# Seven products for three pairs in the second feed-forward's first group, with a new head, tail and addresses

## The chip, the core and the metric

The kernel runs on one core of a Trainium2 chip. A core has five engines that run side by side, each through its own list of instructions in order: PE (TensorE, matrix products), DVE (VectorE), ACT (ScalarE), POOL (GpSimd) and SP (SyncE, which here only issues DMAs). They meet by semaphores: an instruction waits until others have counted far enough, and everything behind it in its engine's list waits too. The metric is the device time of one execution in microseconds (us). Lines are written L288 for line 288 of the kernel before.

## The reference

One encoder layer on x of 256 tokens by 2048 features, all in float32:

```python
x = x + 0.5 * swiglu_ffn(rms_norm(x, ffn1_norm), ffn1_w_in, ffn1_w_out)
h = rms_norm(x, mix_norm); p = h @ w_mix_in          # convolution group | gated group
x = x + concat(rms(conv_group(p)), rms(gated_group(p))) @ w_mix_out
x = x + memory_cross_attention(rms_norm(x, xattn_norm), rms_norm(mem, mem_norm), w_q, w_kv, w_o)
x = x + 0.5 * swiglu_ffn(rms_norm(x, ffn2_norm), ffn2_w_in, ffn2_w_out)
return rms_norm(x, final_norm)

def swiglu_ffn(h, w_in, w_out):                      # w_in 2048 x 11264, w_out 5632 x 2048
    gate, up = split(h @ w_in, 2)
    return (silu(gate) * up) @ w_out
```

What is to be known of it here: the last product of the attention is o @ w_o; its result is added to x, and then the second feed-forward begins, whose first product needs the normalised x. The normalisation divides each token by the root of its mean square, so the division can be done after the product, on the result.

## The kernel before

*Products.* A float32 product is made of three fast ones. Each weight tile of 128 x 1024 comes by DMA into `raw` (512 KB), ACT rounds it into the high half of `hl` (the cast, L339 in the feed-forwards, L112 elsewhere), DVE subtracts that from the tile into the low half (L340, L113), and x is split in the same way into `x_hl`. The product is high by high, low by high and high by low, added up in PSUM. `raw` has four buffers and `hl` three; the feed-forwards add two more `hl` in a tile `ring`, and five more raws in a tile `spare`.

*A feed-forward* (class `FeedForward`) makes h in 11 groups of 512 gate and 512 up columns. A group goes over 16 steps of k, 128 features each, two to a pair p. In a pair marked C, `eight` makes 24 matmuls of 128 x 512 (`by_two`: two token halves, two column halves, three parts, two steps). In a pair marked S, `seven` makes a product of two by two blocks with seven block products in place of eight: 21 matmuls. It needs sums of weight blocks, which DVE makes (L388, L389, L394, L401) and which are then cast like a weight, and sums of x blocks, the forms, which `sides` makes once (two scalings L368 on ACT, four small operations L370 to L375 on DVE, a cast and a subtraction, L120 and L121). A group's pattern is SCSCSCCC. The seven block products are combined at the end of the third S pair (a copy of block product 1 on ACT, L439, and four additions on DVE, L440 to L443) and of the group. Three steps of k in each group take a weight tile `hl_s` whose low half a DMA on POOL's queue adds up (`summed`, L358 and L359).

*The first group* of each feed-forward does not follow the pattern: it goes through all 16 steps as `by_two` does, 192 matmuls, and beside it `sides` makes the forms at k = 6, 9 and 12. At k = 13 the root of the mean square is made (`rms_cols` and `inverse_root`, with a load of another function table on ACT, L204), and then the table for Silu is loaded again.

*The head.* In the first feed-forward, x comes in transposed pieces (L532), weights in raws, the constants `pv` in two pieces, and x once more in four chunks of 512 KB, which ACT squares in place (L525) in raw buffers at k = 5, 7, 9 and 11.

*Attention's last product.* For f = 0 to 15 (128 features each) `gemm_t` makes o @ w_o, of which parts for f = 0 to 3 were begun before, and `residual` adds it to x on DVE (L251, twice), scales the result by the norm's gain into `x_hl` (L239 on ACT, L240 on DVE) and adds up its squares (L212 or L215, L216). o lies in a tile `o_hl` with the tag S2; `spare` of the second feed-forward has the same tag, so the same room.

*The end.* The last product of the second feed-forward is made token half by token half; `add_up` adds and squares, and `give` makes the root from the four sums of squares and scales and stores the half.

*Order.* The order on each engine is set when the kernel is built, by a scheduler with its own estimates of time, from the dependences between tiles and the order in which the program is written. `issue_after` in the program holds an instruction back in it.

## Time and profile before

| what | value |
| --- | --- |
| runs | 2108.7, 2107.7 and 2108.14 us; median 2108.14 |
| profiled execution | 2108.84 us, of which the span of the profile is 2107.04 |
| mean granted clock of PE | 0.998 |
| busy | PE 2084.5 us (99%), DVE 1576.8 (75%), ACT 1161.6 (55%), POOL 67.7 (3%) |
| matmuls recorded | 9764 |
| bytes moved by DMA | 442.34 MB, 210 GB/s over the span |
| stages | first feed-forward's first group from 7.1 to about 57 us, attention's last product until 1386.3, second feed-forward's first group until about 1430, last matmul at 2096.6 |

In the rows that follow, a time at a row's start is in us from the beginning of the span. A row of a timeline gives start, busy time, engine, line, operation, output and inputs, shape, count, and in brackets how long the engine was idle before it and what released it. A row of a window table gives for each engine busy time and count, then the granted clock, the share of the DMA engines' time and GB/s. A row of groups gives count, busy us and mean ns of one.

### The profile page before, as it was taken

What the parts mean: (1) busy time and instruction counts of PE and PEld (TensorE: products, weight loads), DVE (VectorE), ACT (ScalarE), POOL (GpSimd) and SP (SyncE); (2) the same over time, 40 slices, a digit from 0 to 9 for tenths busy, and PEclk for the clock granted to TensorE, in tenths of its full rate; (3) what the DMA queues carried; (4) which work ended last, traced back from release to release, by engine and by line L of the source; (5) the groups of instructions that cost most, each with busy time, mean ns of one, the idle gap of its engine ahead of it and who ended that gap; (6) DMA issues with size and microseconds to landing.
All of it is one profiled execution on the core that took longest, in us unless ns stands there. A gap on an engine that the chain in (4) does not pass through costs nothing.

```text
span 2107.0 us, 26590 instructions
## 1 busy us (share of the span) xinstructions
PE 2084.5 (99%) x9764; PEld 1738.5 (83%) x9764; DVE 1576.8 (75%) x2215; ACT 1161.6 (55%) x1450; POOL 67.7 (3%) x83
## 2 busy tenths in 40 slices
PE   8999999999999999999999999999999999999998
PEld 6888888888888888888888888888888888888886
DVE  6888888876655589889877665777888887787754
ACT  7666566645544454445665454556665666554443
POOL 0000000000000000000000000000000000000000
PEclk9999999999999999999999999999999999999999
DMA  9778777855666676666565543686787778556664
GB/s 360 230 227 257 229 238 245 263 167 169 216 198 188 206 236 200 190 176 185 176 201 185 186 154 111 206 281 191 231 259 247 232 229 250 178 160 202 197 192 149
DMA packets 122244, 442.34 MB, mean 210 GB/s; under 512 B 13697, under 2 KB 13825, under 8 KB 121729
## 3 DMA queue, kind: packets, MB, share of 16 engines
q1 hardware_dynamic: 113184, 407.35, 58.8%
q0 software_dynamic: 8640, 32.51, 8.5%
q8 instruction: 76, 1.25, 0.2%
q10 hardware_dynamic: 288, 0.79, 0.1%
q14 instruction: 56, 0.45, 0.1%
HBM read 438.49 MB, written 2.10 MB: 209 GB/s over the span
## 4 chain that ended last, share of the span: by engine, by line
PE 84%; issue 11%; DMA 2%; ACT 1%; POOL 1%; DVE 1%; SPq 0%; POOLq 0%; ACTq 0%
PE acc L172 12%; PE acc L173 12%; PE acc L171 12%; PE acc L125 9%; PE acc L289 7%; PE acc L288 7%; PE acc L291 7%; PE acc L126 4%; PE acc L277 2%; PE acc L276 2%; PE acc L275 2%; PE aux L263 1%; PE acc L1066 1%; PE acc L1065 1%; PE acc L1067 1%
## 5 line engine op out<-in xcount | busy, mean ns | idle before, releaser
L113 DVE TENSOR_TENSOR hl<-raw,hl 128x1024 fp32r<-128x1024 f32 (+1 forms) x402 | 488.6, 1216 | 282.5 <-ACT hl L112 281.1
L112 ACT CAST hl<-raw 128x1024 fp32r<-128x1024 f32 (+1 forms) x402 | 419.7, 1045 | 481.6 <-PE acc L173 289.3
L339 ACT CAST hl<-spare 128x1024 fp32r<-128x1024 f32 (+1 forms) x135 | 131.8, 993 | 95.5 <-DVE spare L389 38.5
L340 DVE TENSOR_TENSOR hl<-spare,hl 128x1024 fp32r<-128x1024 f32 (+1 forms) x135 | 154.4, 1150 | 35.8 <-ACT hl L339 34.2
L288 PE MATMUL acc<-hl,x_hl 128*128 128x512 f32 x408 | 144.2, 394 | 9.7 <-ACT hl L339 9.7
L289 PE MATMUL acc<-hl,x_hl 128*128 128x512 f32 x408 | 149.9, 395 | 0.0
L340 DVE TENSOR_TENSOR hl<-raw,hl 128x1024 fp32r<-128x1024 f32 (+1 forms) x101 | 113.9, 1131 | 45.9 <-ACT hl L339 44.3
L339 ACT CAST ring<-spare 128x1024 fp32r<-128x1024 f32 (+1 forms) x99 | 97.2, 988 | 68.9 <-DVE spare L389 26.9
L340 DVE TENSOR_TENSOR ring<-spare,ring 128x1024 fp32r<-128x1024 f32 (+1 forms) x99 | 112.9, 1145 | 19.9 <-ACT ring L339 18.8
L291 PE MATMUL acc<-hl,x_hl 128*128 128x512 f32 x408 | 127.5, 392 | 0.0
L339 ACT CAST hl<-raw 128x1024 fp32r<-128x1024 f32 (+1 forms) x101 | 97.7, 977 | 51.8 <-PE acc L291 16.1
L172 PE MATMUL acc<-hl,x_hl 128*128 128x512 f32 x256 | 100.5, 392 | 0.2 <-DVE hl L113 0.2
L172 PE MATMUL acc<-hl,m_hl 128*128 128x512 f32 x256 | 100.4, 392 | 0.0
L173 PE MATMUL acc<-hl,m_hl 128*128 128x512 f32 x256 | 100.2, 391 | 0.0
L173 PE MATMUL acc<-hl,x_hl 128*128 128x512 f32 x256 | 99.8, 390 | 0.0
L288 PEld LDWEIGHTS acc<-hl,x_hl 128*128 128x128 f32 x408 | 76.8, 189 | 25.9 <-ACT hl L339 10.1
L289 PE MATMUL acc<-ring,x_hl 128*128 128x512 f32 x248 | 93.1, 389 | 0.0
L288 PE MATMUL acc<-ring,x_hl 128*128 128x512 f32 x248 | 91.2, 390 | 0.0
L171 PE MATMUL acc<-hl,m_hl 128*128 128x512 f32 x256 | 91.2, 393 | 0.0
L289 PEld LDWEIGHTS acc<-hl,x_hl 128*128 128x128 f32 x408 | 77.2, 190 | 16.9 <-DVE hl L340 1.1
L291 PEld LDWEIGHTS acc<-hl,x_hl 128*128 128x128 f32 x408 | 77.5, 190 | 16.4
L125 PE MATMUL acc<-x_hl,hl 128*128 128x512 f32 x256 | 91.0, 398 | 0.0
(359 smaller groups left out, 5173.9 us busy)
## 6 DMA issues: line engine op xcount, KB each, us to landing
spare<-in_ffn_w_in SPq DMA_DIRECT2D x192, 512.0 KB, 6.4
raw<-in_ffn_w_out SPq DMA_DIRECT2D x176, 512.0 KB, 3.8
raw<-in_ffn_w_in SPq DMA_DIRECT2D x160, 512.0 KB, 6.3
hl_s<-in_ffn_w_in POOLq DMA_DIRECT2D x44, 512.0 KB, 7.3
raw<-in_w_mix_vg SPq DMA_DIRECT2D x32, 512.0 KB, 4.6
raw<-in_w_k SPq DMA_DIRECT2D x32, 512.0 KB, 4.0
raw<-in_w_v SPq DMA_DIRECT2D x32, 512.0 KB, 4.4
raw<-in_w_mix_out SPq DMA_DIRECT2D x32, 512.0 KB, 4.6
```

The source lines that it names most:

```text
L112: nc.scalar.copy(out=hl[:, 0, :size], in_=raw[:, :size])
L113: newest[0] = nc.vector.tensor_tensor(out=hl[:, 1, :size], in0=raw[:, :size], in1=hl[:, 0, :size].bitcast(F32), op=ALU.subtract)
L125: nc.tensor.matmul(acc, lhsT=w_hi, rhs=x_hl, start=first, stop=False, skip_group_check=True)
L126: nc.tensor.matmul(acc[:, 0], lhsT=w_lo, rhs=x_hl[:, 0], start=False, stop=last, skip_group_check=True)
L171: nc.tensor.matmul(acc[t], lhsT=x[:, 0, s], rhs=hi[:, k], start=k0 + k == 0, stop=False)
L172: nc.tensor.matmul(acc[t], lhsT=x[:, 0, s], rhs=lo[:, k], start=False, stop=False)
L173: nc.tensor.matmul(acc[t], lhsT=x[:, 1, s], rhs=hi[:, k], start=False, stop=k0 + k == nk - 1)
L288: nc.tensor.matmul(acc[t][g], lhsT=x[:, 0, s], rhs=hi[:, cols[g]], start=(t, g) in first, stop=False)
L289: nc.tensor.matmul(acc[t][g], lhsT=x[:, 0, s], rhs=lo[:, cols[g]], start=False, stop=False)
L291: nc.tensor.matmul(acc[t][g], lhsT=x[:, 1, s], rhs=hi[:, cols[g]], start=False, stop=last)
L339: nc.scalar.copy(out=hl[:, 0, :n], in_=raw[:, :n])
L340: newest[0] = nc.vector.tensor_tensor(out=hl[:, 1, :n], in0=raw[:, :n], in1=hl[:, 0, :n].bitcast(F32), op=ALU.subtract)
```

## The change

The changed kernel differs in four things.

1. *First group of the second feed-forward.* It is made by `group(0, ...)`, as the others are: three S pairs of 21 matmuls in place of 24. The root comes inside it, before the last pair. The forms are now made beside attention's last product, at f = 1, 5 and 9, in a `wraw` buffer; the tile `ring` is allocated there.
2. *Head.* The first feed-forward's gains and the first 128 features of x come in one DMA on ACT's queue, the first weight tile in two halves; eleven matmuls of ones run on PE before the first real one. The chunks of x to be squared go into tiles h7 to h4 at k = 2, 4, 6 and 8.
3. *Tail.* Three of the four sums of squares are added up ahead of the last product; in `give` the sum of four and one tensor operation with a small operand are replaced.
4. *Addresses and buffers.* `pv` is 64 bytes shorter, and with small fillers all large tiles (x_hl, ring, spare, raw, hl, h0 to h7) begin at 0 mod 128 where they began at 64. The sums of weight tiles have raw buffers of their own, taken out of the ring of raws (9 become 8, later 7), and are issued after the next step's cast.

Line numbers in the rows of the changed kernel are its own: L372 and L373 are cast and subtraction in the feed-forwards, L115 and L116 elsewhere, L252 and L253 the gain, L225 and L228 the squares, L265 the residual, L323 to L328 the forms, L409, L410, L415 and L422 the sums of weight blocks, L468 to L472 the combination, L392 and L393 the passes for `hl_s`, L217 the root.

ACT's list where attention's last product begins its f loop, in the kernel before (the L112 of 512 is for f = 2, the two of 1024 behind it for f = 3 and 4):

```order
L120 CAST o_hl<-acc 128x256 x4
L112 CAST hl<-raw 128x512
L112 CAST hl<-raw 128x1024 x2
L239 ACTIVATE x_hl<-xT,pv 128x256
L212 ACTIVATE ss<-xT 128x256
L112 CAST hl<-raw 128x1024
L239 ACTIVATE x_hl<-xT,pv 128x256
L215 ACTIVATE sq<-xT 128x256
```

The same place in the changed kernel, ACT:

```order
L123 CAST o_hl<-acc 128x256 x4
L252 ACTIVATE x_hl<-xT,pv 128x256
L225 ACTIVATE ss<-xT 128x256
L323 ACTIVATE raw<-xT,pv 128x256
L252 ACTIVATE x_hl<-xT,pv 128x256
L228 ACTIVATE sq<-xT 128x256
L323 ACTIVATE raw<-xT,pv 128x256
L115 CAST hl<-raw 128x512
L115 CAST hl<-raw 128x1024
L123 CAST ring<-raw 128x4x128
```

Gain, squares and form of f = 0 and of f = 1 now stand ahead of the cast for f = 2.

DVE's list at the end of the last product and the beginning of the second feed-forward, in the kernel before:

```order
L240 SCALAR_TENSOR_TENSOR x_hl<-xT,pv,x_hl 128x256
L216 TENSOR_TENSOR ss<-ss,sq 128x256
L340 TENSOR_TENSOR ring<-raw,ring 128x1024
L340 TENSOR_TENSOR hl<-raw,hl 128x1024
L251 SCALAR_TENSOR_TENSOR xT<-acc,xT 128x256 x2
L340 TENSOR_TENSOR hl<-raw,hl 128x1024
```

And in the changed kernel, DVE (the two L265 are the residual of f = 15, `spare` is the tile in o_hl's room):

```order
L373 TENSOR_TENSOR ring<-raw,ring 128x1024
L253 SCALAR_TENSOR_TENSOR x_hl<-xT,pv,x_hl 128x256
L229 TENSOR_TENSOR ss<-ss,sq 128x256
L265 SCALAR_TENSOR_TENSOR xT<-acc,xT 128x256
L409 TENSOR_TENSOR spare<-raw 128x512
L410 TENSOR_TENSOR spare<-raw 128x512
L265 SCALAR_TENSOR_TENSOR xT<-acc,xT 128x256
L415 TENSOR_TENSOR raw<-spare,raw 128x512
L373 TENSOR_TENSOR hl<-spare,hl 128x1024
```

Where plain low halves stood ready, the first weight sums now stand behind the residual of f = 15, and the cast of these sums is what PE's first products of the group wait for.

ACT's list around the root in the second feed-forward's first group, in the kernel before:

```order
L339 CAST ring<-spare 128x1024 x2
L339 CAST hl<-spare 128x1024 x3
L339 CAST ring<-raw 128x1024
L204 ACT_TABLE_LOAD
L204 ACTIVATE rt_11374<-rv_11373 128x2
L339 CAST ring<-raw 128x512
L418 ACT_TABLE_LOAD
```

And in the changed kernel, ACT (L468 is the copy of block product 1 of the third S pair; the first `ring<-raw` behind it is the cast of that pair's second weight tile):

```order
L372 CAST ring<-raw 128x1024
L372 CAST ring<-spare 128x512
L468 COPY spare<-acc 128x512
L372 CAST ring<-spare 128x1024
L372 CAST ring<-raw 128x1024
L217 ACT_TABLE_LOAD
L217 ACTIVATE rt_11417<-rv_11416 128x2
L372 CAST ring<-spare 128x1024
L372 CAST hl<-raw 128x512
L372 CAST hl<-raw 128x1024 x2
```

The copy and the table load now stand among the casts of the third S pair.

The core of the diff:

```diff
+    gx = xt.tile([P, 2 * KD + KD * T], F32, name="gx", tag="x")
+    gains, xT = gx[:, KD:2 * KD], gx[:, 2 * KD:].rearrange("p (k t) -> p k t", t=T)
+    nc.scalar.dma_start(out=gx[:, KD:2 * KD + T], in_=a["gains_x0"])
+    nc.scalar.dma_start(out=xT[:, 1], in_=a["xT"][:, 1])
+    nc.vector.memset(ones, 1.0)
+    idle = pa.tile([P, 2, T], F32, name="aux")
+    for _ in range(WARM):
+        nc.tensor.matmul(idle[:, 0, :P], lhsT=ones, rhs=ones, start=True, stop=True)
...
             self.raws = [spare[:, i * 1024:(i + 1) * 1024] for i in (5, 0, 1, 2, 3)]
+            self.raws_summed = [self.raws.pop()]
...
         def summed(self, at):
-            raw, hl = self.raw(j, k), self.hls[at % len(self.hls)]
+            raw, hl = self.raws_summed[at % len(self.hls)], self.hls[at % len(self.hls)]
+            nc.sync.dma_start(out=raw, in_=self.w_in[j, :, k])
...
             for p, c in enumerate(self.pattern):
+                if p == n - 1 and root is not None:
+                    r = self.rooted(root)
...
+        def rooted(self, root):
+            r = root()
+            nc.scalar.activation(out=st.tile([P, 1], F32, name="warm"), in_=ones[:, 0:1], func=AF.Silu)
+            self.summed(0)
+            return r
+        def early(self, before):
+            self.raw_at += 1
+            self.at += 1
+            raw = wraw.tile([P, 1024], F32, name="raw")
+            hl = whl.tile([P, 2, 1024], F32R, name="hl")
+            halves = [slice(G, 2 * G), slice(0, G)]
+            for s in halves:
+                nc.sync.dma_start(out=raw[:, s], in_=self.w_in[0, :, 0, s])
+            x = before(0)
+            for s in halves:
+                with tc.issue_after(x.ins):
+                    split(hl[:, 0, s], hl[:, 1, s], raw[:, s])
+            return hl
...
-            for k in range(KD):
...
+            if early:
+                acc = token_accs()
+                for k in range(KD):
...
+            else:
+                r = self.group(0, None, root=root)
...
     def x_squares(c):
-        raw = wraw.tile([P, 1024], F32, name="raw")
+        raw = ff.h[7 - c].rearrange("p a b -> p (a b)")
...
-            if k in (5, 7, 9, 11):
-                x_squares(k // 2 - 2)
+            if k in (2, 4, 6, 8):
+                x_squares(k // 2 - 1)
...
+            ring = big.tile([P, 4, 2, 1024], F32R, name="ring", tag="S0")
+            done = [2 * p + 1 for p, c in enumerate(PATTERNS[1]) if c == "S"]
             for f in range(KD):
...
                 residual(acc, f, 1.0, x_hl, "ffn2_norm", ss)
+                if f in done:
+                    raw = wraw.tile([P, 1024], F32, name="raw")
+                    sides(f - 1, lambda k: col("ffn2_norm", k), forms_in(ring)[done.index(f)], raw[:, :512], raw[:, 512:])
...
-        def first_beside(k):
-            if k in (6, 9, 12):
-                ff.sides(k // 3 - 2)
-        turns = ff.run(lambda k: None, first_beside, lambda: rms_cols(ss, D, "r_x2"))
+        turns = ff.run(lambda: rms_cols(ss, D, "r_x2"))
...
-            nc.vector.reduce_sum(out=tot, in_=sums[:, t], axis=AX.X)
-            nc.scalar.activation(out=s, in_=tot, func=AF.Sqrt, scale=1.0 / D, bias=eps)
-            nc.vector.tensor_scalar(out=v, in0=tot, scalar1=1.0 / D, scalar2=RMS_EPS, op0=ALU.mult, op1=ALU.add)
+            last = sums[:, t, 3:4]
+            nc.scalar.activation(out=s, in_=last, func=AF.Sqrt, scale=1.0 / D, bias=most[t])
+            nc.vector.tensor_scalar(out=v, in0=last, scalar1=1.0 / D, scalar2=most[t], op0=ALU.mult, op1=ALU.add)
             nc.vector.reciprocal(out=r, in_=s)
-            nc.vector.scalar_tensor_tensor(out=r, in0=v, scalar=r, in1=s, op0=ALU.mult, op1=ALU.add)
+            nc.vector.tensor_scalar(out=r, in0=v, scalar1=r, scalar2=s, op0=ALU.mult, op1=ALU.add)
```

124 lines of the change are left out of this document (68 added, 56 removed).

## The prediction

> **What bounds the kernel now.** I read the page first, for the share of each engine; then the waits of TensorE (PE) and a table of windows over the first 58 us; then the timelines at the beginning and the end of attention's last product and the groups of instructions in a steady group of the second feed-forward; last the timeline of the end.
>
> ```profile
> span 2107.0 us, 26590 instructions
> PE 2084.5 (99%) x9764; PEld 1738.5 (83%) x9764; DVE 1576.8 (75%) x2215; ACT 1161.6 (55%) x1450; POOL 67.7 (3%) x83
> 1472.00:1514.00 42.00, 42.00 (x187) 34.79 (x186) 33.94 (x41) 24.87 (x28) 2.58 (x3) 1.00 0.80 237
> ```
>
> PE is busy for 99% of the span, and in a steady group of the second feed-forward (third line: PE 42.00 of 42 us, DVE 33.94, ACT 24.87, clock 1.00) nothing else ends last. So the time is the matmuls, times their pace, plus PE's few holes. A change pays by fewer matmuls or fewer holes, and costs by new holes. The old holes lie at the beginning:
>
> ```profile
> PE acc L288 <- ACT hl L339: 9.7, 2, 7.1
> 7.10:11.50 4.40, 4.39 (x11) 3.47 (x11) 3.91 (x6) 3.38 (x5) 0.00 (x0) 1.00 1.01 365
> 11.50:41.80 30.30, 30.30 (x134) 24.87 (x133) 21.86 (x34) 25.65 (x39) 1.88 (x2) 1.00 1.03 389
> 41.80:45.10 3.30, 0.72 (x3) 0.30 (x3) 0.63 (x3) 2.41 (x4) 0.00 (x0) 1.00 1.04 380
> 45.10:49.00 3.90, 3.90 (x11) 2.73 (x11) 2.95 (x7) 2.10 (x3) 0.00 (x0) 0.56 1.04 310
> 6.01 1.04 ACT L339 CAST hl<-raw 128x1024 fp32r<-128x1024 f32 x1 [0.47 <-DMA raw<-in_ffn_w_in]
> 42.69 1.06 ACT L525 ACTIVATE raw<-raw 128x1024 f32<-128x1024 f32 x1 [1.92 <-DMA raw<-in_x]
> 44.82 1.50 PE L288 MATMUL acc<-hl,x_hl 128*128 128x512 f32 x4 [2.58 <-ACT hl L339]
> ```
>
> The first row: in the first 60 us PE waited twice for a cast, 9.7 us in all, the longer time 7.1 us from the start. The window rows give length, PE busy (count), weight loads, DVE, ACT, POOL, granted clock, DMA share, GB/s. 134 matmuls in 30.30 us are 0.226 us each; that is the warm pace. The second hole is at 44.82: ACT sat behind the fourth chunk of x squares (L525), whose DMA kept it until 42.69, so the cast that PE needed came late. PE was idle for 2.58 us, and the window after it has a granted clock of 0.56.
>
> **The change, part by part: gains.** *Head.* The first cast waits for a 512 KB raw, until 6.01. Now its first half comes alone (256 KB less at 365 GB/s: 0.7 us), the 256 KB pair of x columns ahead of it is replaced by a smaller load on ACT's queue (some 0.35 us), and the cast is of half a tile, 0.62 instead of 1.04 (the 128x512 row below): the first matmul at 7.11 - 0.7 - 0.35 - 0.4 = 5.6, a gain of 1.5. Eleven idle matmuls run before it, so the first window should be at full pace: 4.40 - 11 x 0.226 = 1.9. The x squares now go through idle h tiles, early in SP's queue: the hole goes, 3.30 - 3 x 0.226 = 2.6, and its slow clock, 3.90 - 11 x 0.226 = 1.4. That is 7.4. Against it: chunks of x now stand ahead of raws 3, 4 and 5 in SP's queue, while the DMA share is 1.01 to 1.04. A chunk takes 512 KB / 389 GB/s = 1.3 us; a step of k brings 640 KB (1.65 us) and PE needs 12 x 0.226 = 2.7 us for it, so about one late raw remains, 0.4 (0 to 1.7, more than a whole chunk). Head: -7.0, between -5.7 and -7.4.
>
> *Matmuls.* Three pairs of 21 instead of 24: -9 x 0.226 = -2.0 us. This is the whole arithmetic gain of the title.
>
> *Tail.*
>
> ```profile
> 2095.60 0.16 DVE L1025 TENSOR_REDUCE f_tot<-sums 128x1 f32<-128x4 f32 x1 [0.79 <-ACT sq L1019]
> 2095.79 0.15 DVE L1027 TENSOR_SCALAR f_v<-f_tot 128x1 f32<-128x1 f32 x1
> 2096.32 0.64 DVE L1029 SCALAR_TENSOR_TENSOR f_r<-f_v,f_r,f_s 128x1 f32<-128x1 f32 x1
> 2097.48 1.15 ACT L1036 ACTIVATE spare<-spare,f_r 128x1024 f32<-128x1024 f32 x1
> 2098.64 0.63 ACT L1019 ACTIVATE sq<-spare 128x512 f32<-128x512 f32 x1
> 2100.11 0.60 DVE L1029 SCALAR_TENSOR_TENSOR f_r<-f_v,f_r,f_s 128x1 f32<-128x1 f32 x1
> ```
>
> The sum L1025 leaves the chain (0.19 from start to start), and L1029 becomes a tensor-scalar (0.64 or 0.60 against the 0.15 of L1027). Both tokens' chains are in series, since token 1's squares (2098.64) wait for token 0's L1036. 2 x 0.19 + 0.49 + 0.45 = 1.27; POOL's product and DVE's add stay where they are, so I take -1.2 (-0.6 to -1.3). Gains: 7.0 + 2.0 + 1.2 = 10.2.
>
> **The change, part by part: new holes.** *Beginning of the last product.* The two forms of the first S pair are made at f = 1, and with them both gains and squares of f = 0 and 1 move on ACT ahead of the cast of f = 2's weights, which in the kernel before stood ahead of all of them. Now the order is a ring: gain of f = 1 waits for DVE's residual (L265), that for PE's last matmul of f = 1, and PE's next matmul, f = 2, for the cast behind the gain.
>
> ```profile
> 1313.76 0.62 ACT L112 CAST hl<-raw 128x512 fp32r<-128x512 f32 x1 [3.16 <-PE acc L126]
> 1314.42 0.69 DVE L113 TENSOR_TENSOR hl<-raw,hl 128x512 fp32r<-128x512 f32 x1 [3.35 <-ACT hl L112]
> 1315.06 1.23 DVE L251 SCALAR_TENSOR_TENSOR xT<-acc,xT 128x256 f32<-128x256 f32 x3
> 1316.96 0.50 ACT L239 ACTIVATE x_hl<-xT,pv 128x256 fp32r<-128x256 f32 x1
> 1317.37 0.40 ACT L212 ACTIVATE ss<-xT 128x256 f32<-128x256 f32 x1
> ```
>
> Two residuals 0.8, gain 0.41 to its successor, squares 0.4, the form's scaling 0.4, the cast 0.62, and 0.2 for PE's pipeline: 2.8 us in which PE has nothing. The low half (0.69, behind DVE's parts of the forms) makes the second matmul late by 0.4. +3.2 (2.5 to 4). In the kernel before, PE goes through here without a wait, because the cast was at 1313.76.
>
> *From the last product to the first group.*
>
> ```profile
> 1386.34 0.28 PE L126 MATMUL acc<-o_hl,hl 128*128 128x256 f32 x1
> 1386.46 0.62 PE L288 MATMUL acc<-hl,x_hl 128*128 128x512 f32 x2
> L388 DVE TENSOR_TENSOR spare<-raw 128x512 f32<-128x512 f32 x1 | 0.7, 682 | 0.0
> L389 DVE TENSOR_TENSOR spare<-raw 128x512 f32<-128x512 f32 x1 | 0.7, 684 | 0.0
> L339 ACT CAST hl<-spare 128x1024 fp32r<-128x1024 f32 x7 | 7.3, 1053 | 7.8 <-DVE spare L389 5.1 <-DVE spare L394 1.3 <-ACT ring L339 0.7
> L340 DVE TENSOR_TENSOR hl<-spare,hl 128x1024 fp32r<-128x1024 f32 x7 | 8.5, 1221 | 1.3 <-ACT hl L339 1.1
> spare<-in_ffn_w_in SPq DMA_DIRECT2D x5, 512.0 KB, 6.3
> ```
>
> Before, the first feed-forward matmul follows the last product's last one in 0.12 us, on tiles cast ahead. Now the first products need the sums of the first pair, which lie in `spare`; that tile shares its room with o_hl and comes free only with the last product's last matmul. Then: 0.26 to DVE, a residual 0.41, two sums 0.68 + 0.68 (less some 0.1 overlap), a cast 1.05: 3.0 us, less the 0.12 that passes anyway, 2.9. Low half late: 0.4. The raws in `spare`, and the own raw of the sums, can be issued only then, and take 6.3 us to land (median of five in a row); the last of them is some 1.3 us a piece later, near 9. Behind it on ACT stand two passes for the sums and two casts that the second S pair needs, 4.2 in all: 13.2 us after the last product. PE has 21 + 24 matmuls until there, 10.2, and 3.3 of waits: 13.5. That is too close, and I count 0.7 for it. +4.0 (2.9 to 6.5).
>
> *The group's last S pair.* In a steady group ACT's order here is copy of product 1, then casts. Now the root's table load and its small operations stand between those casts, and the copy, which waits for product 1, stands ahead of the cast of the second raw, which products 2 and 3 of the same pair need. The price of a load:
>
> ```profile
> L418 ACT ACT_TABLE_LOAD x1 | 1.3, 1283 | 0.0
> L442 DVE TENSOR_TENSOR spare<-spare,aux 128x512 f32<-128x512 f32 x1 | 0.7, 681 | 0.0
> ```
>
> From product 1's end DVE needs the copy 0.6, two of the group's additions 1.36, a low half 1.22, one more addition 0.68, the second raw's low half 1.22: 5.1 us, while PE has some 12 matmuls (2.7 us): 2.4. Then a fourth addition and the difference for product 4 (1.36) run on DVE, and ACT, after its load (1.28) and a cast that waits for PE's buffer (1.05), makes the half cast (0.62): another 1.6 for product 4, 0.75 for the cast behind it, 0.2 for its low half. +5.0 (2.5 to 6.5). Cover: in the group before, loads and root lay beside a group whose tiles were cast far ahead.
>
> *Clock.* Two of these holes are as long as the one at 44.82 (2.8 and 2.9 against 2.58), which cost 1.4 in slow clock. After the second, PE waits for others anyway, so I charge 1.4 once (0 to 2.8). The Trainium skill, "TensorE: Matmul & The Clock Gate", section "What's actually happening", lets the array go cold after an idle window of about 3.4 us; by that neither hole would do it and the sum would be 1.4 lower. The row of 0.56 behind a hole of 2.58 us speaks against it.
>
> The forms themselves (9 ACT and 15 DVE instructions) are not new, they are moved beside the last product, where the window below shows both engines with room; and the sums' own raw buffers cost nothing as long as 8 or 7 raws keep ahead.
>
> ```profile
> 1330.00:1352.00 22.00, 22.00 (x128) 19.24 (x128) 16.57 (x27) 11.60 (x17) 0.00 (x0) 1.00 0.59 191
> ```
>
> **Sum.** -10.2 + 3.2 + 4.0 + 5.0 + 1.4 = +3.4. The profiled execution took 2108.84 (its span 2107.04); the median of the three runs is 2108.14, 0.7 lower, and I set the sum on that: 2111.5. All terms at their good ends: 2108.1 - 10.7 + 2.5 + 2.9 + 2.5 + 0 = 2105.3; at their bad ends 2108.1 - 8.3 + 4 + 6.5 + 6.5 + 2.8 = 2119.6. A change under 0.2% (4.2 us) is about what cannot be told from none.
>
> **Rivals.** *Faster: the pace changes.* All large tiles now begin at 0 mod 128, where they began at 64. A row of 2048 bytes at 64 touches 17 pieces of 128 bytes, at 0 only 16. If reading these pieces sets the pace, 0.226 becomes 0.213, and 9764 x 0.013 = 127 us less, some 100 if not all of them gain: about 2000. For it: the pace is the same in every stage, whatever the other engines do, as if something of the read itself set it. Against it: no row shows another address. It decides over everything else from a gain of 0.001 us a matmul on. The section "Back-to-back issue gap" of that page of the Trainium skill gives N/2.4 + 2.5 ns, 216 ns for 512 columns; no run here shows that. Chance 0.10.
>
> *Faster, small: the last S pair doesn't stall.* If its casts come ahead of the copy's wait in time, as in steady groups (PE 42.00 of 42), the 5.0 go, and with the shorter lag the 0.7 for late raws: 2105.8; with a warm clock 2104.4. Against it: copy and cast are in one queue. Chance 0.20.
>
> *Slower: the raws set the end.* If the five raws in `spare` land 6.3 us after the last product, and each waits in the queue, PE lags by the 6.5 of the upper end, and the head keeps one chunk's 1.7: 2111.5 + 2.5 + 1.3 = 2115.3, and with both holes cold 2116.7. It is slower by over 0.2% from 0.9 us on. Chance 0.20.
>
> **How the numbers follow.** Forecast 0.50, the pace 0.10, no stall 0.20, late raws 0.20. Faster by over 0.2% (under 2103.9): the pace and a part of the second rival that takes other terms' good ends too, 0.10 + 0.09, and 0.04 of the forecast: 0.23. Slower (over 2112.4): 0.20 of the third and 0.17 of the forecast, 0.37. Within: 0.40. The range 2101 to 2118 holds all but the pace and some of the ends of the others.
>
> **What would show it.** Right: first L288 at 5.6 with clock 1.00, no hole before 49, first group's end near 50; a PE idle of near 3 us for an ACT cast in the last product's third tile and another at its end; two to four waits of 0.5 to 2.5 us around the root. Wrong: PE without idle at these three places, or 512-column matmuls at another pace than 0.226.

## The result, and the profile after

The change makes the kernel slower: 2124.78 us against 2108.42 us (medians of six runs each, 2123.07 to 2126.46 and 2107.70 to 2111.19), a ratio of 1.0076 with a 95% interval of [1.0063, 1.0088]. The forecast was 2111.5 with a range up to 2118. The profiled execution of the changed kernel has a span of 2121.30 us, 14.26 more than before's 2107.04; the working below goes by these two. (By the medians the difference is 16.4: the execution that was profiled is the shortest of the changed kernel's six.) First the page's heads:

```profile
span 2121.3 us, 26651 instructions
PE 2098.7 (99%) x9777; PEld 1742.3 (82%) x9777; DVE 1594.3 (75%) x2243; ACT 1169.9 (55%) x1458; POOL 67.8 (3%) x83
```

PE's share is 99% as before, though its busy time is 14.2 us longer with nine products fewer. (The count is 13 higher all the same, since the eleven idle matmuls at the start leave 22 records, over some 4 us.) So the share alone tells nothing: a matmul at half clock, or one that takes a few ns more, counts as busy. What tells is the start of the same instruction in the two traces. The third column of times is of the experiment e1 below, which differs from the changed kernel in addresses alone.

| start of (us) | before | after | lag | e1 | lag |
|---|---|---|---|---|---|
| first real matmul | 7.11 | 5.39 | -1.72 | 5.65 | -1.46 |
| first Silu, first feed-forward (ACT) | 58.33 | 50.59 | -7.74 | 50.72 | -7.61 |
| first residual behind the first feed-forward (DVE) | 1100.98 | 1095.87 | -5.11 | 1093.19 | -7.79 |
| residual of f = 0, last product (DVE) | 1315.06 | 1309.58 | -5.48 | 1306.78 | -8.28 |
| residual of about f = 9 (DVE) | 1353.38 | 1353.23 | -0.15 | 1350.45 | -2.93 |
| first S pair of the second feed-forward's third group (PE) | 1472.13 | 1483.68 | +11.55 | 1481.10 | +8.97 |
| first addition of the second feed-forward's last product (DVE) | 1918.13 | 1932.21 | +14.08 | 1927.38 | +9.25 |
| last matmul (PE) | 2096.64 | 2112.13 | +15.49 | 2105.88 | +9.24 |
| end of the span | 2107.04 | 2121.30 | +14.26 | 2115.1 | +8.1 |

The table parts the span in three: steps between 1310 and 1450 us, which both kernels on the right have; a drift in the two feed-forwards, which the changed kernel has over e1 (2.7 us until 1101, none from there to 1483, 3.7 behind); and gains at both ends. The very first row is not exact: among the runs with the new head the first real matmul starts between 5.31 and 5.77.

*The head.* Windows of the changed kernel, columns as in the prediction:

```profile
5.00:11.50 6.50, 6.04 (x26) 4.61 (x25) 6.29 (x13) 6.24 (x12) 0.00 (x0) 1.00 1.02 357
11.50:41.80 30.30, 30.24 (x133) 24.44 (x132) 24.34 (x43) 27.36 (x43) 1.01 (x1) 1.00 1.03 396
41.80:49.00 7.20, 7.20 (x33) 5.99 (x32) 5.06 (x8) 3.40 (x4) 0.00 (x0) 1.00 1.03 420
```

The first real matmul starts at 5.39, and where PE had 2.58 us of nothing and then 0.56 of its clock it now is busy for 7.20 of 7.20 us. (The 1.00 in the first row proves nothing by itself: e11 below has it too, while its first matmuls start at half the pace.) The starts of the same matmuls show where the head gains most of its 7.7: 1.7 us until the first, 1.5 over the next ten, 2.4 by the hole, and 1.8 by the slow clock behind it.

*The three holes.* PE's waits of the changed kernel from 1300 to 1430 us (in us: total, times, longest):

```profile
PE acc L289 <- ACT hl L372: 4.5, 2, 2.9
PE acc L128 <- ACT hl L115: 3.0, 1, 3.0
PE acc L290 <- DVE ring L373: 1.8, 1, 1.8
PE acc L289 <- ACT ring L372: 0.4, 1, 0.4
PE acc L290 <- DVE hl L373: 0.4, 1, 0.4
PE acc L134 <- DVE o_hl L124: 0.3, 1, 0.3
PE acc L129 <- DVE hl L116: 0.3, 1, 0.3
PE aux L289 <- ACT hl L372: 0.2, 1, 0.2
PE acc L302 <- ACT hl L372: 0.2, 1, 0.2
```

Before, the same window has one row:

```profile
PE acc L131 <- DVE o_hl L121: 0.3, 1, 0.3
```

Without this wait for o_hl, which both have, the changed kernel's are 10.8 us. The first is the ring in the last product. Its timeline, in order of time:

```profile
1309.58 1.71 DVE L265 SCALAR_TENSOR_TENSOR xT<-acc,xT 128x256 f32<-128x256 f32 x4 [3.99 <-PE acc L129]
1311.62 0.49 ACT L252 ACTIVATE x_hl<-xT,pv 128x256 fp32r<-128x256 f32 x1
1312.02 0.40 ACT L228 ACTIVATE sq<-xT 128x256 f32<-128x256 f32 x1
1312.32 0.49 ACT L323 ACTIVATE raw<-xT,pv 128x256 f32<-128x256 f32 x1
1312.72 1.55 ACT L115 CAST hl<-raw 128x512 fp32r<-128x512 f32 x2
1313.37 0.50 PE L128 MATMUL acc<-o_hl,hl 128*128 128x512 f32 x1 [3.00 <-ACT hl L115]
1313.41 0.68 DVE L116 TENSOR_TENSOR hl<-raw,hl 128x512 fp32r<-128x512 f32 x1
```

The cast of f = 2 (L115 at 1312.72) stands behind gain, square and form of f = 1, which stand behind the residual, and PE sits idle until its end: 3.00 us. What it costs beyond the waits stands in the windows behind each hole, where the third column from the end is the granted clock (1.00 before the holes):

```profile
1313.50:1317.80 4.30, 4.03 (x14) 3.18 (x15) 4.17 (x7) 2.33 (x3) 0.00 (x0) 0.64 0.56 164
1389.40:1393.00 3.60, 3.20 (x8) 2.16 (x9) 3.60 (x6) 2.77 (x5) 0.00 (x0) 0.55 1.03 407
1415.90:1423.00 7.10, 3.13 (x11) 1.57 (x10) 6.39 (x13) 4.81 (x7) 0.00 (x0) 0.82 0.51 140
1423.00:1427.20 4.20, 4.20 (x10) 3.33 (x11) 3.80 (x5) 1.82 (x2) 0.00 (x0) 0.50 0.90 297
```

The clock fell behind every one of the three, to 0.64, 0.55 and 0.50. In the last window ten matmuls take 4.20 us in place of 2.27.

To count all of it I set each stretch of the matmul records against a steady pace: time from the first start to the last, less 226.7 ns for each matmul of 512 columns and 120 for each of 256. This excess holds waits, slow clock and small delays. A few records are missing, and what a missing record adds is in it too; the stretches of before show how little that is. In the changed kernel the stretches go from 1306 to 1346, from 1383 to 1414 and from 1414 to 1435 us, in the others (e1 to e9 are the experiments below) over the same matmuls, as far as they have them.

| excess over the pace (us) | before | after | e1 | e5 | e6 | e7 | e9 | e8 |
|---|---|---|---|---|---|---|---|---|
| beginning of the last product | 0.12 | 5.45 | 5.47 | 0.65 | 5.70 | 5.98 | 0.12 | 0.14 |
| its end and the group's beginning | 0.02 | 6.25 | 6.69 | 5.81 | 0.58 | 6.96 | 0.55 | 0.02 |
| third S pair and the group's rest | 0.45 | 7.84 | 7.90 | 8.87 | 7.24 | 2.56 | 4.56 | 0.45 |

After less before is 18.9 us: 10.8 of waits by name, and 8.1 of slow clock with small delays. One thing in the table is of another kind: in the profiled executions of e5, e6 and e7 (and e11) the 512-column products of `o_hl` with `hl` take about 236 ns from start to start through the whole last product, in place of 231 to 233, which makes them 1.2 to 1.3 us longer in all. No run shows why. Their spans below hold this time, the spans that they are set against do not.

*The drift.* Groups of instructions with `hl_s` (the operand that is kept per pair of weight tiles) from 1440 to 1840 us: count, busy us, mean ns of one. The changed kernel:

```profile
L302 PE MATMUL acc<-hl,x_hl 128*128 128x512 f32 x159 | 55.0, 390 | 0.0
L302 PE MATMUL acc<-hl_s,x_hl 128*128 128x512 f32 x116 | 46.0, 396 | 0.0
L305 PE MATMUL acc<-hl_s,x_hl 128*128 128x512 f32 x116 | 36.6, 395 | 0.0
```

and before, in the same window:

```profile
L288 PE MATMUL acc<-hl_s,x_hl 128*128 128x512 f32 x112 | 43.6, 389 | 0.0
L291 PE MATMUL acc<-hl_s,x_hl 128*128 128x512 f32 x112 | 36.1, 389 | 0.0
```

The products on hl kept their 390 ns, those on hl_s went from 389 to 395 and 396. From start to start (matmul records) it is 226.7 to 227.2 ns before, for every operand, and after 235.3, 229.0 and 233.1 ns for the three products on `hl_s`. In the feed-forwards' own last products it is 232.4 on `hC` and 232.7 on `hl_s`, which lies beside it, and still 227 to 228 on the tiles of h that lie elsewhere (`hA`, `hB`).

*The end.* From the last matmul to the end of the span it is 9.18 us where it was 10.40.

### The profile page after: what moved, and what is told of

Same layout as the page of the kernel before. It is cut to its first block, busy times and chain, and to the rows that moved or that the text cites. A ratio compares the mean times of both kernels' runs of the same rounds, so it can differ in the third digit from the quotient of the medians.

```text
span 2121.3 us, 26651 instructions
## 1 busy us (share of the span) xinstructions
PE 2098.7 (99%) x9777; PEld 1742.3 (82%) x9777; DVE 1594.3 (75%) x2243; ACT 1169.9 (55%) x1458; POOL 67.8 (3%) x83
## 5 line engine op out<-in xcount | busy, mean ns | idle before, releaser
L116 DVE TENSOR_TENSOR hl<-raw,hl 128x1024 fp32r<-128x1024 f32 (+1 forms) x402 | 488.3, 1216 | 279.9 <-ACT hl L115 279.0
L115 ACT CAST hl<-raw 128x1024 fp32r<-128x1024 f32 (+1 forms) x402 | 419.2, 1045 | 476.2 <-PE acc L176 294.5
L373 DVE TENSOR_TENSOR hl<-spare,hl 128x1024 fp32r<-128x1024 f32 (+1 forms) x131 | 150.3, 1151 | 28.9 <-ACT hl L372 25.8
L372 ACT CAST hl<-spare 128x1024 fp32r<-128x1024 f32 (+1 forms) x131 | 129.4, 994 | 74.2 <-PE acc L305 25.7
L303 PE MATMUL acc<-hl,x_hl 128*128 128x512 f32 x396 | 142.4, 393 | 0.3 <-DVE hl L124 0.2
L373 DVE TENSOR_TENSOR hl<-raw,hl 128x1024 fp32r<-128x1024 f32 (+1 forms) x108 | 121.2, 1127 | 26.9 <-ACT hl L372 25.6
L372 ACT CAST hl<-raw 128x1024 fp32r<-128x1024 f32 (+1 forms) x108 | 103.8, 975 | 63.4 <-PE acc L305 25.3
L302 PE MATMUL acc<-hl,x_hl 128*128 128x512 f32 x396 | 136.9, 393 | 0.4 <-ACT hl L123 0.2
L305 PE MATMUL acc<-hl,x_hl 128*128 128x512 f32 x396 | 123.8, 391 | 0.0
L372 ACT CAST ring<-spare 128x1024 fp32r<-128x1024 f32 (+1 forms) x82 | 81.3, 993 | 55.2 <-issue 21.8
L373 DVE TENSOR_TENSOR ring<-spare,ring 128x1024 fp32r<-128x1024 f32 (+1 forms) x82 | 93.9, 1148 | 18.7 <-ACT ring L372 17.4
L175 PE MATMUL acc<-hl,x_hl 128*128 128x512 f32 x256 | 100.5, 393 | 0.2 <-DVE hl L116 0.2
L176 PE MATMUL acc<-hl,x_hl 128*128 128x512 f32 x256 | 99.8, 390 | 0.0
L128 PE MATMUL acc<-o_hl,hl 128*128 128x512 f32 x256 | 90.9, 398 | 3.0 <-ACT hl L115 3.0
L128 PE MATMUL acc<-y_hl,hl 128*128 128x512 f32 x256 | 90.5, 399 | 0.0
L174 PE MATMUL acc<-hl,x_hl 128*128 128x512 f32 x256 | 89.9, 391 | 0.0
L302 PEld LDWEIGHTS acc<-hl,x_hl 128*128 128x128 f32 x396 | 74.5, 189 | 17.0 <-ACT hl L372 1.0
L303 PEld LDWEIGHTS acc<-hl,x_hl 128*128 128x128 f32 x396 | 74.3, 189 | 16.8 <-DVE hl L373 0.8
```

The costliest lines, as they stand in the source:

```text
L115: nc.scalar.copy(out=hl[:, 0, :size], in_=raw[:, :size])
L116: newest[0] = nc.vector.tensor_tensor(out=hl[:, 1, :size], in0=raw[:, :size], in1=hl[:, 0, :size].bitcast(F32), op=ALU.subtract)
L128: nc.tensor.matmul(acc, lhsT=w_hi, rhs=x_hl, start=first, stop=False, skip_group_check=True)
L174: nc.tensor.matmul(acc[t], lhsT=x[:, 0, s], rhs=hi[:, k], start=k0 + k == 0, stop=False)
L175: nc.tensor.matmul(acc[t], lhsT=x[:, 0, s], rhs=lo[:, k], start=False, stop=False)
L176: nc.tensor.matmul(acc[t], lhsT=x[:, 1, s], rhs=hi[:, k], start=False, stop=k0 + k == nk - 1)
```

## The experiments

Two questions are parted: what makes the drift (e1, e2, e4, e10, e12), and what the group, its three holes and the head are worth (e3, e5 to e9, e11). Times are medians with lowest and highest; before ran beside each on the same chip, with 2106.77 to 2107.10 as its median there. Since ten runs of one kernel on one chip spread over 3 to 5 us, spans of the profiled executions are given beside them. e1 to e4, e5 to e8 and e9 to e12 ran on three different chips.

**e1, all large tiles at one place mod 256.** In the changed kernel `gx` is 128 bytes longer than the tile it replaces, and so x_hl, ring, hl and raw begin at 0 mod 256, but hl_s, h0 to h7 and hC at 128. A filler of 128 bytes behind `gx` brings all to 0.

```diff
+    xt.tile([P, 32], F32, name="pad_128")
```

> The changed kernel with 128 unused bytes behind gx, so that hl_s, h0 to h7, hC and the attention's tiles begin at 0 mod 256 (they begin at 128 mod 256 in the changed kernel, all other large tiles at 0 mod 256); the order on every engine is the same. Theory A, a row at 128 mod 256 is read more slowly: matmuls that read hl_s or hC, which took about 235 and 232 ns from start to start, go back to 227, and the time falls by 4 to 7 us to about 2119. Rival B, the slower pace comes from the sums' own raws and the later issue of their DMAs: nothing moves, 2124.8. The three holes around attention's last product stay in both.

Measured 2117.35 (2116.21 to 2119.21), 1.0049 [1.0032, 1.0066] of before; span 2115.1 against 2121.3. The groups in the same window:

```profile
L303 PE MATMUL acc<-hl_s,x_hl 128*128 128x512 f32 x116 | 45.1, 389 | 0.0
L306 PE MATMUL acc<-hl_s,x_hl 128*128 128x512 f32 x116 | 35.9, 389 | 0.0
```

The products on hl_s are back at 389 ns, and the drift is gone from the table above (lag +8.97, +9.25, +9.24 over the last 620 us). Nothing else was changed, and every engine has the same order, so the addresses cost 6.2 us by the traces, 7.4 by the medians. Set start against start, 5.8 of the 6.2 lie in the some 1,090 matmuls that mix hl_s or hC with a tile at the other place (single waits left out): 2.9 in those of hl_s with x_hl, 1.9 of hl with hC, 1.0 of hl with hl_s. The three holes are as they were (table of the excess).

**e2, the kernel before with all tiles at 128 mod 256.**

```diff
+    const.tile([P, 16], F32, name="pad_64")
```

> The kernel before with 64 unused bytes behind pv: all large tiles move from 64 mod 256 to 128 mod 256, order the same. Theory A, an address at 128 mod 256 costs some 6 to 8 ns a matmul: nearly all of the 9764 matmuls are slower, the time rises by 50 to 75 us to 2160 to 2185. Rival B, addresses have no part: 2108. Rival C, only the region in which hl_s and hC lie matters, since they are slow there at 128 mod 256 while others are not: up by 4 to 7 us, to 2112 to 2115.

Measured 2106.77 (2105.66 to 2110.95), 1.0003 [0.9993, 1.0012]: no change.

```profile
L289 PE MATMUL acc<-hl_s,x_hl 128*128 128x512 f32 x113 | 44.0, 389 | 0.0
L292 PE MATMUL acc<-hl_s,x_hl 128*128 128x512 f32 x114 | 36.7, 389 | 0.0
```

hl_s lies here at the very address that it has in the changed kernel, and its products take 389 ns. So neither 128 mod 256 is slow in itself, nor that place in the memory. What is left is how the operands of one product lie to each other.

**e4, the changed kernel moved by 64 bytes.** The same filler, so x_hl, hl and ring stand at 64 mod 256 as before, hl_s and hC at 192: still 128 apart.

```diff
+    const.tile([P, 16], F32, name="pad_64")
```

> The changed kernel with 64 unused bytes behind pv: all large tiles begin at 64 mod 128 as before the change (most at 64 mod 256, hl_s, h0 to h7 and hC at 192 mod 256), order the same. Theory A (128 mod 256 is slow, nothing else): 2118 to 2120. Rival C, what matters is that hl_s and hC stand 128 off the others: 2124 as in the changed kernel. Rival D, 0 mod 128 is worse everywhere: below 2117.

Measured 2124.67 (2122.23 to 2125.88), 1.0080 [1.0065, 1.0095], as slow as the changed kernel, and the first row of its hl_s groups reads as there:

```profile
L303 PE MATMUL acc<-hl_s,x_hl 128*128 128x512 f32 x116 | 46.0, 396 | 0.0
```

So 0 mod 128, which the change took pains for, is neither good nor bad; the distance of 128 bytes is what costs.

**e12, the kernel before with 128 bytes between.** The converse: the same distance put into the kernel that never had it.

```diff
+    xt.tile([P, 32], F32, name="pad_128")
```

> The kernel before with 128 unused bytes behind xT: hl_s, h0 to h7, hC and the attention's tiles move to 192 mod 256, all other large tiles stay at 64 mod 256; order the same. Theory C, operands 128 apart mod 256: matmuls with hl_s or hC slow to 235 and 232 ns, about +6 us: 2113. Rival, the change's own raws are needed for it: 2107.

Measured 2117.04 (2114.01 to 2118.04), 1.0049 [1.0035, 1.0062]; span 2112.2.

```profile
L289 PE MATMUL acc<-hl_s,x_hl 128*128 128x512 f32 x112 | 44.3, 395 | 0.0
L292 PE MATMUL acc<-hl_s,x_hl 128*128 128x512 f32 x113 | 37.3, 395 | 0.0
```

Start to start they are 234.2, 229.0 and 233.5 ns, and 232.5 with hC: the pattern of the changed kernel, in the kernel before. The loss is 5.2 us by the spans and 10.3 by the medians, where 6 were expected; e1's were 6.2 and 7.4. Start against start, the same three kinds of products lose 5.9 us here and gained 5.8 there. The cause of the drift is thereby shown from both sides. e10, on a distance of 64, stands below, since it builds on e3.

**e3, the first group by two again.** The changed kernel with head, ends and addresses, but with the second feed-forward's first group as before, forms made at k = 6, 9 and 12 inside it.

```diff
-                if f in done:
-                    raw = wraw.tile([P, 1024], F32, name="raw")
-                    sides(f - 1, lambda k: col("ffn2_norm", k), forms_in(ring)[done.index(f)], raw[:, :512], raw[:, 512:])
-        turns = ff.run(lambda: rms_cols(ss, D, "r_x2"))
+        def first_beside(k):
+            if k in (6, 9, 12):
+                ff.sides(k // 3 - 2)
+        turns = ff.run(lambda: rms_cols(ss, D, "r_x2"), lambda k: None, first_beside, early=True)
```

> The changed kernel with the second feed-forward's first group as it was before (all 16 steps by two, forms made inside it, root at k = 13); head, tail and addresses as changed. Theory: the three holes and the slow clock behind them go, about 5.5 at the beginning of the last product and 12.6 around the group, and the 2 us of saved matmuls are lost: 2124.8 - 5.5 - 12.6 + 2.0 = 2108.7. Rival, the holes move elsewhere since the order changes: above 2115.

Measured 2107.51 (2106.07 to 2109.48), 0.9998 [0.9989, 1.0008]; span 2106.5. From 1300 to 1460 us PE waits once, for o_hl:

```profile
PE acc L134 <- DVE o_hl L124: 0.3, 1, 0.3
```

So the group's new form costs 14.8 us by the spans (17.3 by the medians), though it saves 2.0 us of matmuls. With the group undone the changed kernel equals the one before: what head and tail gain (8.9) goes for the drift, which is still in it. e8 gives 8.3 to 9.0 for that; 5.8 of the 9.0 lie in the products that mix, and 1.8 in waits for the DMA of hl_s (2.3 us in e3, 0.5 in e8).

**e8, e3 with e1's filler.** Head and ends alone, and one address mod 256 for all.

```diff
+    xt.tile([P, 32], F32, name="pad_128")
```

> Head and tail of the change alone: the second feed-forward's first group as it was before, all tiles at 0 mod 256. Theory: head -7.7 and tail -1.1 are gains that nothing takes back once all operands have the same address mod 256: 2107.1 - 8.8 = 2098, or up to 2101 if the sums' own raws make more waits for hl_s, as in the plain group run (3.0 us against 1.3). Rival, the addresses matter only beside the S pairs: 2107.5 as in that run.

Measured 2099.22 (2098.70 to 2100.64), 0.9963 [0.9951, 0.9976]; span 2097.5. This is the best of all and beats both kernels: by 0.37% the one before.

**e5, the forms later** (on e1). The forms of the three S pairs are made at f = 5, 8 and 11, when their columns of x have long been there and casts stand ready.

```diff
-            done = [2 * p + 1 for p, c in enumerate(PATTERNS[1]) if c == "S"]
+            pairs = [2 * p for p, c in enumerate(PATTERNS[1]) if c == "S"]
+            done = [5, 8, 11]
-                    sides(f - 1, ...
+                    sides(pairs[done.index(f)], ...
```

> As the run with all tiles at 0 mod 256 (2117.4), but the forms of the three S pairs are made at f = 5, 8 and 11 of attention's last product instead of f = 1, 5 and 9. Theory: the hole in its third tile is a ring through ACT's order at f = 1 and goes with its slow clock, 5.3 us: about 2112. Rival, the forms' work has no room beside this product wherever it stands: the hole is found at f = 5, 8 or 11 again, above 2115.

Measured 2110.93 (2108.57 to 2113.35), 1.0017 [1.0007, 1.0026]: 6.4 under e1 by the medians, 3.8 by the spans (5.1 without the slower products of o_hl).

```profile
1300.00:1330.00 30.00, 29.67 (x171) 25.68 (x171) 23.96 (x49) 19.17 (x33) 0.00 (x0) 1.00 0.58 191
```

PE is busy for 29.67 of 30 us at clock 1.00: the first hole is gone with its slow clock, while the other two stay (table of the excess; the third is 1.0 longer). The ring was made by where the form of the first pair stood.

**e6, the first sums in another tile** (on e1). The sums of the first pair go to a raw tile and no more to the one that shares its room with o_hl.

```diff
-            sums = self.sums
+            sums = self.sums if self.at else wraw.tile([P, 1024], F32, name="raw")
```

> As the run with all tiles at 0 mod 256 (2117.4), but the first S pair's weight sums of the first group go into a wraw buffer and not into spare, which shares its room with o_hl. Theory: the hole at the last product's end is the wait of these sums for o_hl; without it the 2.9 us, the late low half (0.7) and the slow clock (1.5) go: about 2112. Rival, the group's beginning is bound by ACT and DVE anyway, and the time comes back as waits within its first 10 us: 2115 to 2117.

Measured 2108.90 (2108.01 to 2111.09), 1.0011 [1.0002, 1.0020]: 8.5 under e1 by the medians, 5.8 by the spans (7.0 without the slower products), which is more than expected.

```profile
1379.00:1400.00 21.00, 20.92 (x100) 17.06 (x99) 19.18 (x28) 14.91 (x18) 0.89 (x1) 1.00 0.84 300
```

The second hole is gone, excess 6.7 in e1 to 0.6. It hung on that room, as the prediction's chain of residual, two sums and a cast had it.

**e7, the root first** (on e1). Root and table loads ahead of the group, where they are not among the casts of the third S pair; its weight sums stay at their place.

```diff
-                    r = self.rooted(root)
+                    self.summed(0)
-                r = self.group(0, None, root=root)
+                r = root()
+                nc.scalar.activation(out=st.tile([P, 1], F32, name="warm"), in_=ones[:, 0:1], func=AF.Silu)
+                r = self.group(0, r, root=root)
```

> As the run with all tiles at 0 mod 256 (2117.4), but the root of the mean square is made at the group's beginning, so that table load and root don't stand among the casts of the third S pair. Theory: of the waits there (4.9 us and 2.2 of slow clock) the part after the table load goes, some 2.5 us, and the slow clock with it, while the copy ahead of the cast still costs about 2.3; the root costs 0.4 at the beginning: about 2113. Rival, the copy's place alone makes the waits: 2117.

Measured 2112.19 (2110.29 to 2115.02), 1.0023 [1.0014, 1.0032]: 5.2 under e1 by the medians, 3.7 by the spans (5.0 without the slower products).

```profile
1414.50:1422.00 7.50, 6.08 (x24) 3.81 (x23) 7.27 (x10) 5.86 (x7) 0.00 (x0) 1.00 0.59 175
```

The third pair's waits fall to 1.4 us, the longest 0.8, and the clock stays at 1.00: excess 7.9 in e1 to 2.6. So the root among the casts made some two thirds of this hole. Of what is left, 1.2 us wait for ACT's casts and 0.2 for DVE; DVE is busy for 7.27 of 7.50 us there, but that it holds the rest is not shown.

**e9, all three mended** (on e1): e5 and e6 together, and for the third pair the copy of block product 1 held behind the cast that stood in its shadow.

```diff
+                        if j == 0 and root is not None:
+                            with tc.issue_after(self.cast.ins):
+                                nc.scalar.copy(out=p1, in_=b["1"])
```

> The changed kernel, all tiles at 0 mod 256, with forms later, the first pair's sums in a wraw buffer, and in the first group the copy of block product 1 held back behind the next cast. Theory: the holes add up, 2117.4 - 6.4 (forms) - 8.5 (sums) = 2102.5, and the copy behind the cast takes 1.5 to 2 from the waits at the third S pair: 2100.5 to 2101, still above the plain group (2099.2), since DVE has too little room in an S group without hl_s: the 2 us of saved matmuls are eaten. Rival, with the holes mended the saving shows: 2097.

Measured 2101.95 (2100.87 to 2103.93), 0.9978 [0.9969, 0.9986]; span 2099.6. Faster than before, yet 2.1 us behind e8's span, though it has nine matmuls fewer. The window of the group, here and then in e8:

```profile
1378.50:1420.00 41.50, 39.16 (x166) 29.96 (x165) 35.88 (x50) 24.43 (x30) 0.89 (x1) 1.00 0.85 290
```

```profile
1378.30:1425.00 46.70, 46.70 (x211) 38.71 (x210) 34.82 (x53) 29.99 (x38) 0.89 (x1) 1.00 0.77 269
```

e8's PE has no hole in it. In e9 PE lacks 2.3 us and DVE is busy for 86% (35.88 of 41.50), against 75% in e8. What PE waits for is mostly DVE (1.7 of 2.2 us; the three longest rows):

```profile
PE acc L304 <- DVE hl L374: 0.8, 2, 0.6
PE acc L291 <- DVE ring L374: 0.7, 1, 0.7
PE acc L290 <- ACT ring L373: 0.3, 1, 0.3
```

An S pair by seven takes four additions of weight blocks, three low halves of 128x1024 and one of 128x512 on DVE: some 7.1 us, estimated from 0.68 us for each addition and the small low half and 1.22 for each large one, against 21 x 0.227 = 4.8 us on PE. Other groups have steps with hl_s between, whose low half DVE does not make; the first group has none. So three pairs by seven save 2.0 us of PE there and lose about 4.6 (the excess of e9 over e8 in the table; 2.2 of it are waits with a name, the rest delays between matmuls that no row names). That DVE is what sets this loss is argued from its share and these waits; no run relieved DVE alone.

**e10, 64 bytes apart** (on e3): hl_s, h and hC at 192 mod 256 as the others stand at 0, a distance of 64 mod 128.

```diff
+    xt.tile([P, 16], F32, name="pad_64")
```

> As the plain group at 0 mod 256 (2099.2), but hl_s, h0 to h7, hC and the attention's tiles at 64 mod 128 (192 mod 256) while x_hl, ring, hl and raw stay at 0. Theory C1, what costs is a matmul whose two operands lie 128 apart mod 256, and nothing else: 2099. Theory C2, any difference costs, with the same 6 to 9 ns a matmul: 2106 as at a difference of 128.

Measured 2107.05 (2105.64 to 2109.13), 1.0004 [0.9994, 1.0013]; span 2103.8, 6.3 above e8 (7.8 by the medians), from which it differs by the filler alone.

```profile
L303 PE MATMUL acc<-hl_s,x_hl 128*128 128x512 f32 x112 | 44.1, 394 | 0.0
L306 PE MATMUL acc<-hl_s,x_hl 128*128 128x512 f32 x112 | 35.3, 394 | 0.0
```

The three products on hl_s with x_hl now take 233.2 ns from start to start, a little more than at a distance of 128 on the average (232.3). But those of hl with hC and with hl_s take only 229.4 and 229.2, where they take 232.4 and 232.7 at 128. In all, the products that mix lose 4.6 us against e8, and about 1.7 of the 6.3 lie elsewhere. So a distance of 64 costs too, as much as 128 does in one kind of product and less than half of it in the others.

**e11, without the idle matmuls** (on e8).

```diff
-    idle = pa.tile([P, 2, T], F32, name="aux")
-    for _ in range(WARM):
-        nc.tensor.matmul(idle[:, 0, :P], lhsT=ones, rhs=ones, start=True, stop=True)
```

> As the plain group at 0 mod 256 (2099.2) without the eleven idle matmuls at the start. Theory: the first ten matmuls run at half the clock, 2 us: 2101.2. Rival, the DMAs bind the head and a slower start is made good by fewer waits later: 2099.

Measured 2101.80 (2100.74 to 2103.84), 0.9977 [0.9968, 0.9986]; span 2100.2. PE's timeline in e11, and in e8:

```profile
7.87 0.63 PE L301 MATMUL acc<-hl,x_hl 128*128 128x512 f32 x1
8.30 0.54 PE L300 MATMUL acc<-hl,x_hl 128*128 128x512 f32 x1
8.67 0.40 PE L303 MATMUL acc<-hl,x_hl 128*128 128x512 f32 x1
```

```profile
7.42 0.39 PE L303 MATMUL acc<-hl,x_hl 128*128 128x512 f32 x1
7.65 0.39 PE L306 MATMUL acc<-hl,x_hl 128*128 128x512 f32 x1
```

From 7.87 to 8.30 it is 0.43 us from one matmul to the next in e11, and 0.23 only from about 8.67 on; in e8 it is 0.23 at 7.42 already. By the spans and by the medians e11 is 2.6 to 2.7 us behind e8, close to the 2 that were expected, but that is luck. Start against start, e11's eleventh matmul is 1.04 us behind e8's, and at 52 us of the span it is 0.7; 1.3 us more come from the products of o_hl with hl in attention's last product, which are slower in this execution as in e5 to e7, and the rest is scattered. So the eleven idle matmuls are worth about 1 us, of which 0.7 is left behind the first group; the prediction had taken 1.9 for it. e11's first matmul starts 0.16 us earlier than e8's, less than the runs with e8's head differ among themselves.

## Why the prediction was wrong, point by point

The same sum, by the traces:

| term (us) | forecast | measured |
|---|---|---|
| head | -7.0 | -7.7 |
| matmuls | -2.0 | -2.0 (nine fewer; not measured alone) |
| tail | -1.2 | -1.2 |
| three holes, waits | +12.2 | +10.8 |
| slow clock and small delays behind them | +1.4 | +8.1 |
| addresses | none | +6.2 |
| sum | +3.4 | +14.2 (spans: +14.3) |

**Head and tail: right in size.** 5.39 against 5.6 for the first matmul, the hole at 44.82 and its slow clock gone, no late raw to speak of. Two parts were off and made good for each other, which is luck: the pace of the first window was taken at 1.9 and gave 1.5 (about 1 of it by the idle matmuls), and the slow clock behind the old hole was taken at 1.4 and gave 1.8, since the window that it was read from ends while PE is still slow. The tail's terms add up to 1.32, not to the 1.27 that stands there; -1.2 is what came.

**The holes: right in place, cause and nearly in size.** The ring in the last product was forecast at 3.2 and waited 3.0 + 0.3; the step to the first group was 4.0, of which 2.9 + 0.4 and 0.2 came (e6 shows that the shared room was all of it); the third S pair was 5.0 and waited for 1.6 + 1.8 + 0.4 + 0.2. The forecast of raws that come late (0.7) did not come true, and with it falls the rival that set the end by them: no PE row waits for a DMA there. The rival in which the last pair does not stall falls by the row of 1.8.

**The slow clock: the first step that failed, by its size.** The term "charged once" rested on the thought that PE waits for others anyway after the second hole. It hardly does: from the second hole to the third pair it waits for 0.6 us in all, and each hole had its price. By the table of the excess (after less before, less the waits by name: 5.3 - 3.3, 6.2 - 3.5, 7.4 - 4.0) it is about 2.0 behind the first, 2.7 behind the second and 3.4 behind the third, small delays included; the rows of 0.64, 0.55 and 0.50 bear the larger part. The upper end of that term, 2.8, was two holes at 1.4. The third was not even counted as one, since it was thought of as several short waits; 1.8 and 1.6 within 5 us were enough for a clock of 0.50, while e7 and e9, where no single wait is over 0.8 there, kept 1.00. The Trainium skill, "TensorE: Matmul & The Clock Gate", section "What's actually happening", lets the array go cold after an idle window of about 3.4 us. By the letter none of these holes is that long; the trace differs, with a slow clock behind 2.58, 3.0 and 2.9 us, and the measurement decides.

**The addresses: the second step that failed, a term that was missing.** The prediction looked at addresses only as a gain in a rival ("the pace changes", 0.10) and at each tile by itself, 17 pieces or 16. That rival falls: with all operands at 0 mod 256 (e1) a matmul takes what it took at 64. What the change also did, by the 128 bytes that `gx` holds ahead of x, is to put hl_s, h and hC at another place mod 256 than x_hl and hl. The diff shows that prefix, and the text said "all at 0 mod 128", which is true and not enough. No row of before could have priced it, since there all tiles stood alike; but a bound on both sides was due, as for any cost that no row shows.

Of the 10.8 us between forecast and result by the spans, 6.7 are the clock, 6.2 the addresses, and 2.1 go the other way (holes and head). The range, too, was drawn narrower than the sum's own bad ends (2118 against 2119.6), but those would not have held the result either.

**Still open:** why a matmul whose two operands lie 64 or 128 bytes apart mod 256 takes longer, why with 128 the low half of hl_s is slowed by 2 ns where the others are by 6 to 9, and why with 64 it depends on the kind of product. Open as well is what makes the products of o_hl slower in four of the profiled executions. Other distances were not tried, nor was the relation between weights and moving operand parted from others, such as that to what ACT and DVE read and write meanwhile.

## What to carry to other kernels

When work is moved on an in-order engine, ask whether a cast that PE needs next now stands behind something that itself waits for PE: that ring cost 3.0 us of wait, and about 2 more in clock, and was undone by moving the same work four steps on. Charge the clock once for each hole of some 2 to 3 us, never once for all. Waits of up to 0.8 us left it at 1.00 here (e7, e9), so short ones may be cheaper than one long one; no run cut the same wait into pieces. And before a difference between two runs is put down to the edit, set the two traces start against start: in e11 less than half of it lay where the edit was. Before a scheme with fewer matmuls goes into a group, set DVE's time for it against PE's, 7.1 against 4.8 us here; and when a tile changes its size, look at where the tiles behind it come to lie, all of them.

## What the runs showed of the hardware

Matmuls of 128x512 in the feed-forwards' groups run at about 227 ns from start to start when both tiles stand alike mod 256, at 0, 64 or 128 (e1, before, e2). With hl_s and hC apart from the others by 64 they take 233 ns on hl_s with x_hl and 229 on hl with hC (e10), by 128 they take 229 to 235 (after, e4, e12). These are some 1,090 of over 9,700 matmuls, and they lose 4.6 us at 64 and 5.8 to 5.9 at 128, nearly as much as the whole head is worth.

Holes of 2.58, 3.0 and 2.9 us in PE's work, and two waits of 1.8 and 1.6 us close together, were each followed by matmuls at a granted clock of 0.50 to 0.64, which cost 1.8 us behind the first and 2.0 to 3.4 behind the others, small delays included.
